# The four PSUM copies of a chunk step: engine chosen by the scheduler instead of fixed for each head

## Chip, cores and metric

One core of a Trainium2 chip runs the whole program. The metric is the device time of one execution in microseconds; before the change its median is 2306.48 us over 3 runs (2300.24 to 2307.2).

## What is computed

The reference is a two-layer backbone on 512 image tokens and 256 context tokens of width 1024. Layer 0 is an RWKV-7 mixer with 32 heads of 64 (16 pairs of heads) and two scan directions z, layer 1 a Hyena mixer with a long convolution. The change lies in the scan of layer 0, which for each head and direction is

```
def step(s, inp):
    r_t, w_t, k_t, v_t, a_t, b_t = inp
    sa = jnp.einsum('bhvk,bhk->bhv', s, a_t)
    s = s * w_t[:, :, None, :] + sa[..., None] * b_t[:, :, None, :] + v_t[..., None] * k_t[:, :, None, :]
    return s, jnp.einsum('bhvk,bhk->bhv', s, r_t)
```

over the context (256 tokens) and then the image (512), forwards for z = 0 and backwards for z = 1. All is float32.

## The kernel before

The scan is done in chunks of 64 tokens: 4 chunks of context and 8 of image, so 12 steps for each head. The coroutine `chain(r)` (line 1492) runs the 12 steps of a round `r`, which holds two pairs of heads, q = 0 and 1, with both directions z and both heads h of a pair: eight 64x64 problems side by side. There are 8 rounds, one after the other, so 96 steps in all. A step does this:

- eight matmuls of the operand `ar` with `sv` (state and values stacked) give `bx` in one PSUM bank (lines 1522 to 1524);
- two copies bring `bx` into `xs`, one for each head h (lines 1526 and 1527);
- eight matmuls of `xs` with the inverted triangular matrices `tt` give `bu` (lines 1536 to 1538), which two more copies bring into the lower or upper half of `sv[h]` (lines 1539 and 1540);
- eight matmuls of `sv` with `bt` give the state's increment `bs`, which the vector engine adds to the state `sc` and multiplies by the decay into the `sv` of the next step (lines 1541 to 1553);
- for image chunks, matmuls of `ar` and `arb` with `sv` give the output `by`, which `outputs` copies or adds to `yb`.

Both reads of a pair are of one bank: `quad("pa")` hands out half of PSUM bank 2. Head 0 lies in partitions 0 to 63, head 1 in 64 to 127.

Other coroutines run beside it. `fetch(p, g)` (line 1380) issues on SP the loads of the operands for pair p and group g, a group being four steps: 6 transfers `bk<-bkd`, 4 `ar<-ard` and 4 `ar<-zd` (zeros). Its ring `gring` has 4 places, two pairs of two groups; a place comes free after the fourth step of its group (lines 1559 to 1561). `prep(p, g)` (line 1418) makes from them the masked products `ar` and `arb` (vector engine) and the transposes `bt` (TensorE, evicted by ACT or the vector engine). `values` copies the values into the next `sv` (`sv<-vt`, ACT or POOL), `merge` makes `tt` from blocks of `inverse` (vector engine, tiles `lt` and `ltm`), `readout`, `operand` and `out_part` take a finished pair through the group norm (`s`, `yb`, `bo`), the split into `uh` and `ul` and the output projection with the weights `whi` and `wlo`; `adaln` works on the second layer's modulation (`aw`, `arow`).

The order of all instructions is written by a scheduler in the kernel, `run` (line 255). At each turn it takes from every live coroutine the next operation, estimates with `Model` (line 72) when its engine and its operands are free, and emits the one that can start first. An operation may come with alternatives (`alts`): then the way with the earliest estimated end is taken. `copy(eng, out, in_)` (line 403) gives an `ACTIVATE` on ACT (S) or a `COPY` on the vector engine (V); with a tuple of engines it gives alternatives. In `Model` any two accesses to one PSUM bank from different instructions wait for each other (line 120), and its prices and latencies are constants in the class. Every engine runs its instructions in the order in which they were emitted.

All operations are issued through one helper, so the profile has them all under line 58; tiles tell them apart.

Of the kernel before, what the change touches and what calls it, by code (L numbers as in the profile page):

```python
# [239 lines left out]
def net_kernel(ctx: ExitStack, tc: tile.TileContext, I, out, dbg=None):  # L240
    nc = tc.nc
    model = Model()
    V, S, T, G, SP = (Engine(e, n) for e, n in ((nc.vector, "V"), (nc.scalar, "S"), (nc.tensor, "T"), (nc.gpsimd, "G"), (nc.sync, "P")))
# [83 lines left out]
    def tl(pool, name, shape, bufs=1, dt=F32, tag=None):  # L327
        return model.new(pool, name, shape, bufs, dt, tag)
# [45 lines left out]
    def pt(kind):  # L374
        i = turn[kind]
        turn[kind] = (i + 1) % len(kinds[kind])
        return kinds[kind][i]

    def get(kind):

        return (yield from several(kind, 1))[0]
# [21 lines left out]
    def copy(eng, out, in_):  # L403
        if isinstance(eng, tuple):
            op = copy(eng[0], out, in_)
            op.alts = [op] + [copy(e, out, in_) for e in eng[1:]]
            return op
        if eng is S:
            return S.activation(out=out, in_=in_, func=AF.Copy)
        return eng.tensor_copy(out=out, in_=in_)  # L410
# [319 lines left out]
    HR = [slice(0, 64), slice(64, 128)]  # L730
# [568 lines left out]
    def rt(name, shape, bufs=1, dt=F32):  # L1299
        return tl(rx, name, shape, bufs, dt)  # L1300
# [14 lines left out]
    xs = rt("xs", [P, 2, 2, 2, C])  # L1315
# [13 lines left out]
    def two(a, b):  # L1329

        return slice(a, b + 1, b - a) if b > a else slice(a, b - 1 if b > 0 else None, b - a)
# [160 lines left out]
    def chain(r):  # L1492

        ps_ = 2 * r, 2 * r + 1
        QZH = [(q, z, h) for q in range(2) for z in range(2) for h in range(2)]

        def quad(kind):
            return pt(kind).rearrange("p (q z t) -> p q z t", q=2, z=2)

        while not all(p in pr for p in ps_):  # L1500
            yield
        gam, _, ptok = rounds[r]
        gf = gam.rearrange("p q c z -> p q (c z)")
        tt = [tts[p % len(tts)] for p in ps_]
        while not svs:
            yield
        sv, stok = svs.pop(0)
        for h in range(2):
            yield G.memset(sv[h][HR[h]], 0.0)
        sc = rt("sc", [P, 2, 2, C])  # L1510
        yield G.memset(sc, 0.0)
        for n in range(NC):
            g, i = divmod(n, 4)
            base, lc = BASE[g], (i, 3 - i)
            while not all((p, g) in grp for p in ps_):
                yield
            AR, ARB, BT, tok = zip(*[grp[p, g] for p in ps_])
            if n == 4:
                while yring.full():
                    yield  # L1520
                yb = tl(rv, "yb", [P, 2, NCX, C], YB), yring.take(), []
            bx = quad("pa")
            for q, z, h in QZH:
                yield T.matmul(bx[HR[h], q, z, :], lhsT=AR[q][z][h][:, 0, lc[z], :], rhs=sv[h][:, q, z, :], start=True, stop=True)

            for h, e in enumerate((S, V)):
                yield copy(e, xs[HR[h], h], bx[HR[h]])
            if g:

                by, ytok = yield from get("py")  # L1530
                by = by.rearrange("p (q z t) -> p q z t", q=2, z=2)
                for q, z, h in QZH:
                    yield T.matmul(by[HR[h], q, z, :], lhsT=sv[h][:, q, z, :], rhs=AR[q][z][h][:, 1, lc[z], :], start=q + z == 0, stop=False)
            while not all(p in mrgd for p in ps_):
                yield
            bu = quad("pa")
            for q, z, h in QZH:
                yield T.matmul(bu[HR[h], q, z, :], lhsT=tt[q][:, z, base[z] + lc[z], :], rhs=xs[:, h, q, z, :], start=True, stop=True)
            for h, e in enumerate((S, V)):
                yield copy(e, sv[h][HR[h]], bu[HR[h]])  # L1540
            if n < NC - 1:
                bs = quad("pn")
                for q, z, h in QZH:
                    yield T.matmul(bs[HR[h], q, z, :], lhsT=BT[q][z][:, lc[z], HR[h]], rhs=sv[h][:, q, z, :], start=True, stop=True)
                yield V.tensor_tensor(out=sc, in0=bs, in1=sc, op=ADD)
                while not svs:
                    yield
                nsv, ntok = svs.pop(0)
                gv = gf[:, :, two(2 * (base[0] + lc[0]), 2 * (base[1] + lc[1]) + 1)].unsqueeze(3).broadcast_to([P, 2, 2, C])
                for h in range(2):  # L1550
                    yield V.tensor_tensor(out=nsv[h][HR[h]], in0=sc[HR[h]], in1=gv[HR[h]], op=MUL)
                if n < NC - 2:
                    yield G.tensor_tensor(out=sc, in0=sc, in1=gv, op=MUL)
            if g:
                for q, z, h in QZH:
                    yield T.matmul(by[HR[h], q, z, :], lhsT=sv[h][:, q, z, :], rhs=ARB[q][:, h, z, lc[z], :], start=False, stop=q + z == 2)
                ys.todo.append((outputs, r, yb, by, ytok, base, lc, n - 4))
            stok[0] = True
            if i == 3:
                for t in tok:  # L1560
                    t[0] = True
            if n < NC - 1:
                sv, stok = nsv, ntok
        ttfree.update(ps_)
        ptok[0] = True
# [110 lines left out]
    def ready_merge(p):  # L1676
# [4 lines left out]
    ends = [reads, parts, Lane([(out_part, p) for p in range(0, NP, 2)], 1, lambda *a: bool(xp), OB)]  # L1681
    rr = range(NP // 2)
    scans = [Lane([(values, r) for r in rr], 1, lambda *a: True, B_VAL), Lane([(chain, r) for r in rr], 1, lambda *a: bool(zeroed), B_CHAIN),
             Lane([(merge, p) for p in range(NP)], 1, ready_merge, B_MERGE), ys, Lane([(fetch, *x) for x in order], 1, lambda *a: bool(zeroed)), Lane([(prep, *x) for x in order], W_PREP, lambda *a: True, B_PREP), invs]
    G2BIAS = 0
# [405 lines left out]
```

## Time and profile before

| | us |
|---|---|
| median of 3 runs | 2306.48 |
| the profiled execution | 2299.21 |
| its span | 2297.5 |
| busy in the span: TensorE | 2012.7 |
| vector engine | 1650.1 |
| ACT | 1067.1 |
| POOL | 371.8 |

The scan takes about a third of the span, from 835 to 1600 us. Before it lie the projections and the key side of layer 0, behind it the rest of the output projection, the filters and all of layer 1. A row of the timeline gives the start, the duration, the engine, what is written from what, how often in a row, and in brackets how long the engine stood idle before it and what ended that.

### The profile page before, as it was taken

How to read it: one execution, taken by the hardware profiler on the slowest of the kernel's cores; microseconds unless marked ns; L12 is line 12 of the kernel's file. 1: busy time of each engine (PE TensorE's matmuls, PEld its weight loads, DVE VectorE, ACT ScalarE, POOL GpSimd, SP SyncE). 2: the span in 40 equal slices, each digit the busy share in tenths (PEclk: the TensorE clock that was granted, in tenths of full speed). 3: DMA queues.
4: the chain of work that ended last, by engine and by line, in shares of the span. 5: the costliest groups of instructions: out<-in, count | busy, mean ns of one | idle time of the engine just before them, and what ended most of it. 6: DMA issues, size and time to landing. Idle time of an engine off the chain costs nothing. (4 is left out here: it accounts for less than half of the span.)

```text
span 2297.5 us, 53254 instructions
## 1 busy us (share of the span) xinstructions
PE 2012.7 (88%) x21678; PEld 1600.8 (70%) x21678; DVE 1650.1 (72%) x2624; ACT 1067.1 (46%) x1898; POOL 371.8 (16%) x574
## 2 busy tenths in 40 slices
PE   6699899998976787788988889888599999999997
PEld 2488777776754566676776767766477788878786
DVE  1956378999996869767576666766777576767676
ACT  2444588888762333345353453443453333333333
POOL 0400100000001322323223243221322000000000
PEclk8799999999988887999999999999799999999999
DMA  7055757795787884657566575543664423222232
GB/s 246 34 184 188 233 173 233 247 263 181 212 278 216 207 190 111 172 141 188 137 166 149 144 179 140 145 132 111 197 191 156 147 79 106 82 96 94 87 123 75
DMA packets 317628, 369.39 MB, mean 161 GB/s; under 512 B 132387, under 2 KB 203630, under 8 KB 317384
## 3 DMA queue, kind: packets, MB, share of 16 engines
q1 hardware_dynamic: 303752, 330.21, 49.3%
q0 software_dynamic: 13632, 35.78, 5.3%
q8 instruction: 171, 2.80, 0.5%
q14 instruction: 73, 0.60, 0.1%
HBM read 262.79 MB, written 102.30 MB: 159 GB/s over the span
## 5 line engine op out<-in xcount | busy, mean ns | idle before, releaser
L58 PE MATMUL ps<-m,whi 128*128 128x512 f32 (+1 forms) x1536 | 418.5, 374 | 47.7 <-ACT whi L58 19.0
L58 ACT ACTIVATE whi<-wraw 128x512 fp32r<-128x512 f32 x320 | 200.5, 628 | 385.4 <-PE ps L58 288.9
L58 DVE TENSOR_TENSOR wlo<-wraw,whi 128x512 fp32r<-128x512 f32 x320 | 229.6, 719 | 193.7 <-ACT whi L58 191.2
L58 PEld LDWEIGHTS ps<-m,whi 128*128 128x128 f32 x1536 | 262.4, 196 | 105.9 <-ACT whi L58 20.8
L58 PE MATMUL ps<-m,wlo 128*128 128x512 f32 (+1 forms) x768 | 245.8, 370 | 4.6 <-DVE wlo L58 4.5
L58 PE MATMUL ps<-ar,bk 128*64 128x64 f32 (+2 forms) x4096 | 216.7, 243 | 33.3 <-DVE ar L58 17.8
L58 PEld LDWEIGHTS ps<-ar,bk 128*64 128x64 f32 (+1 forms) x4096 | 184.6, 141 | 55.0 <-issue 24.5
L58 PE MATMUL ps<-h1h,whi 128*128 128x512 f32 x512 | 201.8, 394 | 2.4 <-ACT whi L58 1.4
L58 PE MATMUL ps<-h1h,wlo 128*128 128x512 f32 x512 | 201.2, 393 | 0.7 <-DVE wlo L58 0.7
L58 PE MATMUL ps<-h1l,whi 128*128 128x512 f32 x512 | 201.0, 393 | 0.0
L58 PEld LDWEIGHTS ps<-m,wlo 128*128 128x128 f32 x768 | 133.1, 196 | 31.1 <-DVE wlo L58 6.7
L58 DVE TENSOR_TENSOR ar<-ps,cst 64x512 f32<-64x512 f32 (+1 forms) x192 | 114.8, 599 | 22.9 <-PE ps L58 17.9
L58 POOL TENSOR_TENSOR sc<-sc,gam 128x256 f32<-128x256 f32 x80 | 56.4, 705 | 428.0 <-DVE sv L58 420.2
L58 PEld LDWEIGHTS ps<-h1h,whi 128*128 128x128 f32 x512 | 96.7, 189 | 22.1 <-ACT whi L58 1.8
L58 PEld LDWEIGHTS ps<-h1h,wlo 128*128 128x128 f32 x512 | 97.0, 189 | 21.1 <-DVE wlo L58 1.2
L58 PEld LDWEIGHTS ps<-h1l,whi 128*128 128x128 f32 x512 | 96.8, 189 | 20.0 <-DVE h1l L58 0.5
L58 PE MATMUL ps<-sv,bt 128*64 128x64 f32 x1408 | 89.1, 236 | 16.8 <-DVE sv L58 9.5
L58 DVE TENSOR_TENSOR ltm<-lt 128x90 f32<-128x90 f32 (+14 forms) x120 | 81.4, 678 | 29.2 <-DMA wraw<-wg 17.6
L58 ACT ACT_TABLE_LOAD x76 | 97.5, 1283 | 8.1 <-DMA aw<-ada_w 5.9
L58 PEld LDWEIGHTS ps<-sv,bt 128*64 128x64 f32 x1408 | 66.9, 142 | 41.8 <-DVE sv L58 15.8
L58 ACT ACTIVATE sv<-ps 64x256 f32<-64x256 f32 x96 | 36.1, 376 | 125.9 <-PE ps L58 122.2
L58 PE MATMUL ps<-xs,tt 128*64 128x64 f32 x1536 | 68.6, 232 | 28.2 <-DVE xs L58 26.0
(289 smaller groups left out, 4426.4 us busy)
## 6 DMA issues: line engine op xcount, KB each, us to landing
wraw<-wg SPq DMA_DIRECT2D x128, 256.0 KB
wraw<-w SPq DMA_DIRECT2D x128, 256.0 KB
aw<-ada_w SPq DMA_DIRECT2D x96, 256.0 KB
bkd<-bk SPq DMA_DIRECT2D x32, 768.0 KB
ard<-ar SPq DMA_DIRECT2D x32, 640.0 KB
ar<-ard SPq DMA_DIRECT2D x128, 128.0 KB
ar<-zd SPq DMA_DIRECT2D x128, 128.0 KB
wraw<-w_out SPq DMA_DIRECT2D x64, 256.0 KB
```

What stands on the lines that cost most here:

```text
L58: return getattr(self.eng.eng, self.fn)(*self.a, **self.k)
```

## The change

The fixed pair of engines (ACT for head 0, the vector engine for head 1) at both copies becomes a choice for each copy:

```
-            for h, e in enumerate((S, V)):
-                yield copy(e, xs[HR[h], h], bx[HR[h]])
+            for h in range(2):
+                yield copy((S, V), xs[HR[h], h], bx[HR[h]])
...
-            for h, e in enumerate((S, V)):
-                yield copy(e, sv[h][HR[h]], bu[HR[h]])
+            for h in range(2):
+                yield copy((S, V), sv[h][HR[h]], bu[HR[h]])
```

Nothing else is edited, but since the scheduler decides, the order of nearly all later instructions shifts. ACT in the first round, before the change, in three steps (`sv0` and `sv1` are the tiles of head 0 and 1, `ps2` the bank of `bx` and `bu`, `vt` the values):

```order
L58 ACTIVATE arow_7900<-ps7_70 128x128
L58 ACTIVATE xs_6590<-ps2_65 64x256
L58 ACTIVATE sv0_7185<-ps2_65 64x256
L58 ACTIVATE sv0_7989<-vt_6665 64x256
L58 ACTIVATE sv1_7990<-vt_6665 64x256
L58 ACTIVATE xs_6590<-ps2_65 64x256
L58 ACTIVATE m1_8018<-ps7_70 128x384
L58 ACTIVATE sv0_7850<-ps2_65 64x256
```

ACT at the same place after the change:

```order
L58 ACTIVATE xs_6590<-ps2_65 64x256
L58 ACTIVATE arow_7917<-ps7_70 128x128
L58 ACTIVATE xs_6590<-ps2_65 64x256
L58 ACTIVATE sv0_7185<-ps2_65 64x256
L58 ACTIVATE sv1_7186<-ps2_65 64x256
L58 ACTIVATE sv0_7985<-vt_6665 64x256
L58 ACTIVATE sv1_7986<-vt_6665 64x256
L58 ACTIVATE xs_6590<-ps2_65 64x256 x2
L58 ACTIVATE sv0_7850<-ps2_65 64x256
L58 ACTIVATE sv1_7851<-ps2_65 64x256
```

ACT now has both halves of each pair; once a foreign copy (`arow`) stands between them.

The vector engine a little earlier, in the second step of the round (`-` before, `+` after; `ltm` and `lt` belong to `inverse`, `sc` is the state of the same step):

```order
 L58 TENSOR_TENSOR ltm<-lt 128x174
 L58 TENSOR_TENSOR lt<-lt,ltm 128x3x2x29
-L58 COPY xs<-ps_65 64x256
 L58 TENSOR_TENSOR ltm<-lt 128x252
 L58 TENSOR_TENSOR lt<-lt,ltm 128x3x3x28
 L58 TENSOR_TENSOR ltm<-lt 128x324
-L58 STREAM_TRANSPOSE t_7794<-tt_6588 128x384
-L58 COPY sv_7178<-ps_65 64x256
+L58 STREAM_TRANSPOSE t_7799<-tt_6588 128x384
 L58 TENSOR_TENSOR lt<-lt,ltm 128x3x4x27
 L58 TENSOR_TENSOR ltm<-lt 128x390
```

Both copies are gone from the vector engine's queue there; the products of `inverse` stay, and `sc` and the next `sv` come behind them in both.

## Rows read from the trace of the kernel before

**Rows 1.** Stretches: stretch, length, busy us (instructions) per engine, clock, DMA share, GB/s.
```profile
835.00:1600.00 765.00, 658.34 (x13606) 531.53 (x13606) 537.31 (x1013) 321.09 (x651) 231.24 (x384) 0.94 0.59 147
```

**Rows 2.** Tile `sv`: durations ns min/median/max, first and last start us, forms.
```profile
L58 PE MATMUL ps<-sv,ar x1536: 219/222/371, 835.2 to 1594.3; 128*64 128x64 f32 x192
...
L58 ACT ACTIVATE sv<-vt x107: 400/413/419, 855.0 to 1583.1; 64x256 f32<-64x256 f32 x107
L58 ACT ACTIVATE sv<-ps x96: 358/377/379, 851.8 to 1596.6; 64x256 f32<-64x256 f32 x96
L58 DVE COPY sv<-ps x96: 420/427/430, 852.3 to 1597.4; 64x256 f32<-64x256 f32 x96
```

**Rows 3.** Timeline of one clean step at 1120 us.
```profile
1120.61 0.64 PE L58 MATMUL ps<-sv,ar 128*64 128x64 f32 x16
...
1121.29 0.38 ACT L58 ACTIVATE xs<-ps 64x256 f32<-64x256 f32 x1 [3.69 <-PE ps L58]
...
1121.70 0.43 DVE L58 COPY xs<-ps 64x256 f32<-64x256 f32 x1
...
1122.18 0.69 PE L58 MATMUL ps<-xs,tt 128*64 128x64 f32 x16
...
1122.91 0.38 ACT L58 ACTIVATE sv<-ps 64x256 f32<-64x256 f32 x1 [1.25 <-PE ps L58]
...
1123.32 0.43 DVE L58 COPY sv<-ps 64x256 f32<-64x256 f32 x1 [1.20 <-ACT sv L58]
```

**Rows 4.** Timeline of ACT and the vector engine in a step at 1382 us.
```profile
1382.46 0.38 ACT L58 ACTIVATE xs<-ps 64x256 f32<-64x256 f32 x1
...
1382.93 0.67 DVE L58 SCALAR_TENSOR_TENSOR bo<-bo,sg 128x512 f32<-128x512 f32 x1
1383.63 0.43 DVE L58 COPY xs<-ps 64x256 f32<-64x256 f32 x1
```

**Rows 5.** Timeline of ACT and the vector engine in the second step, at 857 us.
```profile
857.50 0.38 ACT L58 ACTIVATE xs<-ps 64x256 f32<-64x256 f32 x1 [1.06 <-PE ps L58]
...
862.67 0.25 DVE L58 TENSOR_TENSOR ltm<-lt 128x90 f32<-128x90 f32 x1 [6.45 <-DMA hkd<-hh]
...
864.05 0.43 DVE L58 COPY xs<-ps 64x256 f32<-64x256 f32 x1
```

**Rows 6.** Tile `xs`, columns as in rows 2.
```profile
L58 ACT ACTIVATE xs<-ps x96: 360/377/380, 836.0 to 1594.6; 64x256 f32<-64x256 f32 x96
L58 DVE COPY xs<-ps x96: 420/427/429, 836.4 to 1595.0; 64x256 f32<-64x256 f32 x96
```

**Rows 7.** Timelines of SP, vector engine, ACT and TensorE around one group boundary.
```profile
1455.05 1.78 SPq L58 DMA_DIRECT2D bk<-bkd  x3
...
1475.62 0.61 SPq L58 DMA_DIRECT2D ar<-zd  x1
...
1486.12 0.85 DVE L58 TENSOR_TENSOR sv<-sc,gam 64x256 f32<-64x256 f32 x2
...
1492.35 0.60 ACT L58 ACTIVATE bt<-ps 128x512 f32<-128x512 f32 x1 [0.77 <-PE ps L58]
...
1492.98 0.67 PE L58 MATMUL ps<-sv,ar 128*64 128x64 f32 x16
```

**Rows 8.** Timeline of ACT: a copy out of PSUM and the next one.
```profile
1100.27 0.38 ACT L58 ACTIVATE sv<-ps 64x256 f32<-64x256 f32 x1 [1.25 <-PE ps L58]
1100.55 0.49 ACT L58 ACTIVATE m<-ps 128x384 f32<-128x384 f32 x1
```

**Rows 9.** Groups of the vector engine, 835 to 1600 us: busy us, mean ns, idle before.
```profile
L58 DVE TENSOR_TENSOR ar<-ps,cst 64x512 f32<-64x512 f32 x124 | 85.3, 688 | 16.3 <-PE ps L58 13.2
...
L58 DVE COPY bt<-ps 128x512 f32<-128x512 f32 x18 | 12.2, 688 | 5.7 <-PE ps L58 5.5
```

**Rows 10.** Groups over the whole span, columns as in rows 9.
```profile
L58 POOL TENSOR_TENSOR sdl<-sf,sdh 128x512 fp32r<-128x512 f32 x16 | 21.3, 1334 | 45.7 <-ACT sdh L58 45.6
```

**Rows 11.** Waits from 835 to 1600 us: total us, times, longest us.
```profile
ACT arow L58 <- PE ps L58: 21.8, 13, 8.4
ACT whi L58 <- PE ps L58: 21.6, 20, 6.3
...
ACT yb L58 <- DVE yb L58: 7.1, 9, 2.9
...
ACT uh L58 <- DVE bo L58: 5.2, 7, 2.2
```

## Prediction

> **What bounds the kernel now.** I read the stages first, then the tiles of the recurrence, then single steps in the timeline.
>
> The table by stretches isolates the recurrence: from 835 to 1600 us, TensorE is busy 658 of 765 us, the vector engine 537 (70%), ACT 321 (42%) [rows 1]. No engine is full. The first matmul of a step starts at 835.2 and the last at 1594.3 [rows 2], so 96 steps take about 8 us each. The order of TensorE is the same in both kernels up to the first of these steps, and both leave the same work behind the last one (two sums and about 18 triples of the output projection). So the stage is what can change; a saving at its end moves all that follows forward.
>
> Inside a step, TensorE waits for two pairs of copies out of PSUM. In the clean step at 1120 us the ACT copy of `xs` starts at 1121.29 and takes 0.38, the vector copy starts at 1121.70, takes 0.43, and the next matmuls start at 1122.18; the pair of `sv` repeats this at 1122.91 and 1123.32 [rows 3]. **The two engines don't work side by side**: the second copy starts when the first has ended; both read one PSUM bank, and in the program the second waits for a semaphore of the first. From ACT's start to the end of the pair it is 0.41 + 0.43 = 0.84 us. So each pair is a serial piece of the recurrence, on two queues.
>
> Often it is longer. At 1382 us ACT starts `xs` at 1382.46, but the vector engine is in its queue's earlier work and starts its half at 1383.63 [rows 4]. At 857 us the wait is 6.5 us: the vector copy stands behind an `ltm` product that waited for a DMA [rows 5]. Counted over the 96 ACT and 96 vector copies of each tile (first and last in [rows 2, 6]), the vector copy starts 0.67 us after ACT's on average, against 0.41 in the clean step: 192 x 0.26 = 50 us of waiting in all.
>
> The steps are not the whole loop. The operands of four steps (a group, two pairs of heads) come through a ring that holds two groups. Their loads start on SP when the group two before has been read: for the group that starts at 1492.98, the loads run from 1455.05 to 1476.2, then the masks and transposes follow, with the last `bt` eviction at 1492.35 to 1492.95, and the recurrence starts right then [rows 7]. It had been ready since 1486.97, when its state products ended [rows 7]: 6.0 us of waiting for operands. So there are two interlocked loops: start of group n = start of group n-2, plus its four steps, plus load and preparation (1492.98 - 1455.05 = 37.9 us). **What a group's steps save counts once in two groups**, 12 times out of 24.
>
> **The change, part by part.** The order of instructions says what the scheduler chose. Of the 96 `xs` copies of each half, 161 of 192 now go to ACT and 31 to the vector engine; of the `sv` copies 177 and 15. That is 162 pairs wholly on ACT (153 of them back to back), 16 wholly on the vector engine and 14 mixed as before.
>
> *The pair.* No row shows two ACT copies of this shape in a row, but ACT's next eviction starts 0.28 us after such a copy: `sv` at 1100.27 takes 0.38 and `m` starts at 1100.55 [rows 8]. So a pair on ACT is 0.28 + 0.38 = 0.66 us instead of 0.84: 162 x 0.18 = 29 us less along the steps. The bounds are 0.76 (no overlap, 13 us) and 0.66; I take 0.66, because the row has the same shape and source. A vector pair is 2 x 0.43 = 0.86, no gain: 16 x 0.02 = 0.3 us, dropped. The mixed pairs stay.
>
> Had the halves run side by side before, a pair would have cost 0.43 us and ACT alone would lengthen it by 0.23: 162 x 0.23 = 37 us along the steps, half of it in the time, 2325. The clean step contradicts it [rows 3], and since the vector copy waits for ACT's semaphore in every pair, it gets no chance of its own. The Trainium skill (TensorEngine Tiling (Array Packing), PSUM Bottleneck) does advise evacuating PSUM with both ScalarE and VectorE; by that rule this change would go the wrong way, and the trace disagrees for two halves of one bank.
>
> *The vector engine's queue.* 162 of 192 pairs no longer pass it: 50 x 162/192 = 42 us at most, none at least. Not all of it goes. In the step at 857 us, the accumulation `sc` of the same step still stands behind the same `ltm` rows, as the order shows, so the stall moves from the copy to `sc`. I take half, 21 us.
>
> Together 50 us along 96 steps, 2.1 us per group. It counts 12 times: **25 us**.
>
> *Load on the engines.* ACT gains 146 copies at 0.38 us, 55 us [rows 2, 6], and 22 `sv<-vt` copies at 413 ns that went to POOL before, 9 us [rows 2]; 27 other evictions (`bt`, `tt`, `vt`, `arow`) leave it, some 11 us. The vector engine loses 146 copies at 427 ns, 62 us [rows 2, 6], and takes the 27 at up to 0.69 us each [rows 9], at most 19 us. So of 765 us ACT stands at about 321 + 55 + 9 - 11 = 374 and the vector engine at about 537 - 62 + 19 = 494. ACT's additions are hidden by its idle time before these copies; if that cover went, they would be paid in the steps (the slower rival below). The vector engine also does the preparation's masks (the long `ar` form alone is 85 us in this stage [rows 9]). It gets back 43 us in 96 steps, about 0.45 us a step; the preparation between the last load and the first step spans 1476 to 1493, two steps, so some 1 us per link, and I take half, as masks also wait for matmuls: 12 x 0.5 = **6 us**. Bounds 0 and 12.
>
> *The rest.* SP issues the same loads; the group's burst of about 21 us doesn't shrink. In the filter stage the scheduler's clocks come out shifted and four `sdl` subtractions go from POOL (1.33 us [rows 10]) to the vector engine, two `swl` the other way; at most 6 x 1.33 = 8 us either way, taken at 0 because matmuls and SP loads lie between them.
>
> **Sum.** 25 + 6 = 31 us off the profiled execution's 2299.2, so 2268. That execution stands 7.3 us below the median of the runs, 2306.5; 31 us off the median gives 2275.5, rounded to **2276 us**.
>
> **The rivals.**
>
> *Swallowed at the group boundary (no change).* If SP doesn't start the loads of group n earlier although group n-2 ends earlier, since weight loads stand ahead in its queue, each saving turns into a longer wait for operands like the 6.0 us at 1487. For it: SP issues one transfer after the other and also carries weights. Against: at 1455.05 the loads start with the last reading of the group before. Time: 2306.
>
> *Passed on in full.* If preparation isn't the limit in most groups, every step counts: 50 + 6 = 56 us, 2250. For it: within a group nothing but the steps decides. Against: the boundary at 1493 waits for `bt`.
>
> *ACT's queue becomes the bound (slower).* Place: nine of the ACT pairs have a foreign instruction between their halves, as the `arow` in the order: two `arow`, two `whi`, two `yb`, three `uh`. Each waits for something outside the step; the longest such waits before are 8.4, 6.3, 2.9 and 2.2 us [rows 11]. All at their longest: 2 x 8.4 + 2 x 6.3 + 2 x 2.9 + 3 x 2.2 = 42 us. If these pass on in full, no vector queue time comes back and the pairs give only their half of 29, the kernel is 42 - 15 = 27 us slower: 2333. It decides once these waits exceed about 15 us. Against: most waits of this kind are far below their longest (13 `arow` waits total 21.8 us [rows 11]), and the first half always stood in this queue.
>
> That the scheduler would keep the old engines is excluded by the counts above.
>
> **How the numbers follow.** 0.3% is about 7 us, what a measurement of this kernel tells from no change. The forecast has a chance of 0.52, in full 0.18, swallowed 0.14, slower 0.16. The first two are faster by over 0.3%: 0.70; the third is the same, the fourth slower. The forecast's own range is the queue term at 0 to 42 us and the preparation at 0 to 12: (29 + 0)/2 = 15 to (29 + 42)/2 + 12 = 48 us, 2259 to 2292. The range from 2246 to 2310 takes in the full and the swallowed case with a few us beyond them and leaves out the slower one.
>
> **What would show it.** Right: two ACT copies 0.28 us apart in each pair; ACT at about 374 and the vector engine at about 494 us in this stage; the first TensorE row of a step closer behind the copies; the stage some 31 us shorter, all else equal. If boundary waits grow beyond 6 us and the stage keeps its length, it is the second case. If ACT's waits inside a pair (before `arow`, `whi`, `yb`, `uh`) add up to tens of us, the slower case holds. The forecast is wrong too if the stage shortens and a later one grows by the same.

## The result, and the profile after

The changed kernel takes 2276.89 us (median of 4 runs, 2273.82 to 2283.02), the kernel before 2306.84 beside it (4 runs). The ratio is 0.9883, with a 95% interval from 0.9858 to 0.9907: 1.2% faster, 27 us by the ratio (21 to 33), 30 us between the two medians. The profiled execution of the changed kernel took 2273.82 us, its span 2272.1, which is 25.4 us less than the span before; the pieces below add up to these 25.4.

The recurrence between 835 and 1600 us, in the columns of [rows 1]:

```profile
835.00:1600.00 765.00, 655.23 (x13612) 528.32 (x13612) 489.66 (x901) 384.11 (x801) 226.48 (x365) 0.94 0.62 152
```

ACT has gained 63 us (321 to 384) and the vector engine lost 48 (537 to 490). The tile `sv` after gives the last step and the copies that moved [rows 2]:

```profile
L58 PE MATMUL ps<-sv,ar x1536: 219/222/369, 835.8 to 1577.9; 128*64 128x64 f32 x192
...
L58 ACT ACTIVATE sv<-ps x177: 377/379/382, 852.6 to 1581.2; 64x256 f32<-64x256 f32 x177
...
L58 ACT ACTIVATE sv<-vt x129: 400/414/419, 854.4 to 1565.5; 64x256 f32<-64x256 f32 x129
```

The steps begin where they did and end 16 us earlier (1577.9 against 1594.3). Cutting both spans at the start of the last step shows that this isn't all. Before, then after (stretch, length, busy us and instructions of PE, PEld, vector engine, ACT and POOL, clock, DMA share, GB/s):

```profile
835.20:1593.70 758.50, 653.16 (x13536) 527.86 (x13536) 532.76 (x1005) 318.07 (x644) 230.11 (x382) 0.94 0.59 148
1593.70:2297.50 703.80, 639.60 (x3008) 520.89 (x3002) 486.30 (x768) 259.61 (x433) 57.89 (x55) 0.96 0.38 121
```

```profile
835.80:1577.20 741.40, 645.60 (x13537) 523.64 (x13537) 481.33 (x888) 372.71 (x784) 221.61 (x360) 0.94 0.62 151
1577.20:2272.10 694.90, 635.85 (x3006) 516.92 (x3002) 480.88 (x768) 260.06 (x434) 55.09 (x53) 0.96 0.38 123
```

The stretch from the first step's start to the last's lost 17.1 us, and the part behind it, whose operations the change doesn't name, lost 8.9. TensorE runs the same number of products in the first stretch, to within one. Its idle time there fell from 105.3 to 95.8 us and its busy time from 653.2 to 645.6, so 9.5 of the 17.1 us are less waiting and 7.6 are the same products done in less time (more on that in the last section). What it waited for there, first before, then after (us in total, times, longest us):

```profile
PE ps L58 <- DVE xs L58: 26.0, 29, 7.1
PE ps L58 <- DVE sv L58: 16.0, 33, 2.2
...
PE ps L58 <- DMA ar<-zd: 7.5, 9, 2.4
...
PE ps L58 <- ACT sv L58: 6.0, 13, 0.6
```

```profile
PE ps L58 <- DVE sv L58: 20.0, 19, 9.7
PE ps L58 <- DMA ar<-zd: 15.4, 15, 2.0
...
PE ps L58 <- ACT xs L58: 6.3, 11, 1.0
...
PE ps L58 <- ACT sv L58: 4.0, 10, 0.6
PE ps L58 <- DVE xs L58: 1.0, 2, 0.6
```

The wait for the `xs` pair went from 26.0 to 7.3 us; the wait for `sv` (its copies, and the product with `gam` on the vector engine that begins the next step's `sv`) went from 22.0 to 24.0. The whole of what the copies could give TensorE was 48 us, and 31 of it are left: 16.7 us less. Its other idle time grew by 7.2 us, the wait for the zero loads `ar<-zd` by 7.9 alone, so that in all it fell by 9.5.

Two places show why so much copy time gives so little. First the `xs` pair at 1121 us of the changed kernel, on ACT and then on TensorE (start, length):

```profile
1121.64 0.78 ACT L58 ACTIVATE xs<-ps 64x256 f32<-64x256 f32 x2 [3.00 <-PE ps L58]
```

```profile
1121.82 0.39 PE L58 MATMUL ps<-whi,uh 128*128 128x512 f32 x1
1122.05 0.40 PE L58 MATMUL ps<-wlo,uh 128*128 128x512 f32 x1
1122.38 0.69 PE L58 MATMUL ps<-ar,sv 128*64 128x64 f32 x16
1122.89 0.64 PE L58 MATMUL ps<-xs,tt 128*64 128x64 f32 x16
```

The pair ends at 1122.42, but its product starts at 1122.89: TensorE's queue has the output projection and the step's output product (`ps<-ar,sv`) in front of it. TensorE lost nothing there, and in this order a shorter pair would have changed nothing.

Second, the long wait of the second step [rows 5], on TensorE before and after:

```profile
864.53 1.12 PE L58 MATMUL ps<-xs,tt 128*64 128x64 f32 x16 [7.07 <-DVE xs L58]
...
869.64 1.54 PE L58 MATMUL ps<-sv,ar 128*64 128x64 f32 x16 [0.47 <-DVE sv L58]
```

```profile
858.06 1.12 PE L58 MATMUL ps<-xs,tt 128*64 128x64 f32 x16 [0.86 <-ACT xs L58]
859.66 1.52 PE L58 MATMUL ps<-sv,bt 128*64 128x64 f32 x16 [0.48 <-ACT sv L58]
870.91 0.45 PE L58 MATMUL ps<-sv,ar 128*64 128x64 f32 x2 [9.73 <-DVE sv L58]
```

The product behind `xs` comes 6.5 us sooner, and the third step starts at 870.91 instead of 869.64: the accumulation `sc` stands behind the same `ltm` rows on the vector engine. After the change these start 3 us later than in [rows 5], behind another DMA (vector engine, changed kernel):

```profile
865.72 0.25 DVE L58 TENSOR_TENSOR ltm<-lt 128x90 f32<-128x90 f32 x1 [9.75 <-DMA wraw<-w_out]
...
869.89 0.42 DVE L58 TENSOR_TENSOR sc<-ps,sc 128x256 f32<-128x256 f32 x1
```

To follow the copies through all 96 steps I summed each piece of a step over them. The time from the first copy's start to the pair's end fell from 210.8 to 163.9 us (`xs` 110.8 to 82.5, `sv` 100.0 to 81.4). From a pair's end to the next product's start it rose from 29.0 to 51.2 us for `xs`; from the `sv` pair's end to the start of the last state product from 55.6 to 63.3, and from there to `sc` from 42.7 to 50.4, all of it in the second step just shown. So of 47 us that the copies lost, the time inside the steps lost 14.6.

### The profile page after: what moved, and what is told of

It reads as the page before. It is cut to its first block, busy times and chain, and to the rows that moved or that the text cites. A ratio compares the mean times of both kernels' runs of the same rounds, so it can differ in the third digit from the quotient of the medians.

```text
span 2272.1 us, 53272 instructions
## 1 busy us (share of the span) xinstructions
PE 2000.0 (88%) x21678; PEld 1591.7 (70%) x21678; DVE 1593.1 (70%) x2507; ACT 1122.1 (49%) x2039; POOL 360.1 (16%) x550
## 5 line engine op out<-in xcount | busy, mean ns | idle before, releaser
L58 PE MATMUL ps<-ar,bk 128*64 128x64 f32 (+2 forms) x4096 | 211.5, 242 | 48.5 <-DVE ar L58 18.7
L58 ACT ACTIVATE sv<-ps 64x256 f32<-64x256 f32 x177 | 67.0, 378 | 94.7 <-PE ps L58 91.3
L58 ACT ACTIVATE xs<-ps 64x256 f32<-64x256 f32 x161 | 60.8, 378 | 86.7 <-PE ps L58 84.9
L58 PE MATMUL ps<-sv,ar 128*64 128x64 f32 x1536 | 79.6, 234 | 21.9 <-DVE sv L58 19.8
```

Source lines behind the costliest of these rows:

```text
L58: return getattr(self.eng.eng, self.fn)(*self.a, **self.k)
```

## The experiments

The table cuts each profiled execution in three: the time inside steps; the waits between groups (at each fourth step, from the end of the product or copy that finishes it to the next step's first product, 23 times); and the tail from the last step's start to the end. Ratios are to the kernel before, from runs on the same chips. The medians of the result, of e1 to e8, of e9 to e11 and of e12 come from separate runs, beside which the kernel before had medians from 2303.55 to 2306.84 us; across these groups the ratios are what can be compared.

| kernel | median us | ratio, 95% interval | in steps | between groups | tail |
|---|---|---|---|---|---|
| before | 2306.84 | 1 | 649.9 | 108.6 | 703.8 |
| changed | 2276.89 | 0.9883 [0.9858, 0.9907] | 635.3 | 106.1 | 694.9 |
| e1 xs only | 2299.69 | 0.9980 [0.9967, 0.9993] | 657.8 | 112.4 | 694.2 |
| e2 sv only | 2304.80 | 0.9999 [0.9981, 1.0018] | 648.8 | 122.5 | 696.7 |
| e3 all on ACT | 2302.49 | 0.9988 [0.9975, 1.0001] | 634.4 | 135.7 | 697.1 |
| e4 exchanged | 2313.84 | 1.0030 [1.0012, 1.0049] | 659.5 | 123.6 | 699.8 |
| e5 before, filter | 2301.32 | 0.9992 [0.9972, 1.0012] | 653.0 | 106.8 | 701.6 |
| e6 changed, filter | 2281.53 | 0.9907 [0.9876, 0.9938] | 639.3 | 105.7 | 696.7 |
| e7 one copy | 2278.07 | 0.9881 [0.9851, 0.9910] | 591.6 | 159.0 | 694.6 |
| e8 latency | 2306.34 | 1.0004 [0.9983, 1.0024] | 620.1 | 131.3 | 693.5 |
| e9 changed, no zeros | 2251.41 | 0.9768 [0.9745, 0.9791] | 626.8 | 90.1 | 696.0 |
| e10 before, no zeros | 2297.63 | 0.9979 [0.9963, 0.9995] | 677.3 | 92.6 | 698.9 |
| e11 e7 and e9 | 2274.65 | 0.9866 [0.9844, 0.9889] | 626.4 | 118.0 | 699.0 |
| e12 before's order, ACT | 2285.57 | 0.9923 [0.9902, 0.9945] | 635.8 | 112.9 | 705.2 |

One profiled execution stands up to 12 us (e8) above or below its kernel's median, so a difference of a few us between two profiles can belong to the executions and not to the kernels.

**Parts of the change, e1 to e4.** From the changed kernel, e1 puts the second pair back, e2 the first; e3 and e4 replace the choice in both pairs:

```
e1:  for h, e in enumerate((S, V)): yield copy(e, sv[h][HR[h]], bu[HR[h]])
e2:  for h, e in enumerate((S, V)): yield copy(e, xs[HR[h], h], bx[HR[h]])
e3:  for h, e in enumerate((S, S)): ...
e4:  for h, e in enumerate((V, S)): ...
```

> Only the two xs copies go to the engine of choice; the sv copies are again one on ACT and one on the vector engine. Theory A (the gain is the time in which the second half waited for the vector engine's queue, plus 0.08 us of a pair): in the trace of the changed kernel the time from the first xs copy to the second fell by 24 us and the second copy itself by 4, against 14 and 4 for sv, so this kernel has 28 of the 46 us and its gain over the kernel before is about 28/46 of 30, 18 us: 2289. Rival B (the new order as a whole, not these copies, is the gain): any edit moves the filter stage and the boundaries of groups by several us either way, and the gain has no such share; it could be 0 or 30.

> Only the two sv copies go to the engine of choice; the xs copies are again one on ACT and one on the vector engine. Theory A: 18 of the 46 us along the steps, so about 12 us less than before, 2295; with the xs half's gain it adds up to the whole change, 30. Rival B: the two halves do not add up to 30.

> All four copies fixed on ACT, no choice. Theory A: 192 pairs on ACT instead of 162, so as the changed kernel or up to 5 us less, 2270 to 2280. Rival C (it is the choice that pays, and ACT's own queue costs when it gets everything): ACT has some 390 of 765 us and every pair then stands behind ACT's other work; 10 us or more over the changed kernel, 2287 or more.

> One fixed engine for each half as before, with the two engines exchanged: half 0 on the vector engine, half 1 on ACT. The pair still passes both queues and the first copy waits for the vector engine's queue. Theory A: no gain, within 8 us of the kernel before, since the pair is 0.43 + 0.38 us and its start waits where its second half waited. Rival B (reshuffle): the edit moves the order as much as the change does, and the time moves by 10 to 30 us.

The halves don't add up: about 5 us and none, where 18 and 12 were expected, and the whole is 30. In e1 the `xs` pair gained what it should (110.8 to 80.4 us over the steps), but the `sv` copies then waited 10 us more for the vector engine and the waits between groups grew. All on ACT gives some 3 us, not clear of none, though its copies are shorter still than the changed kernel's (149 us over the steps against 163.9) and its steps as short (634.4). The time is lost between groups. e4 ends 7 us over before (ratio 1.0030, clear of 1), within the 8 us of theory A and under the 10 of rival B. Its pairs are 45 us shorter over the steps (210.8 to 166.1), and its first copies start 45 us later behind the products that they read (20.7 to 65.8): the wait for the vector engine moved from the second half to the first. But e1 to e3 show that theory A isn't the only cause: rival B was right that edits of the same kind move the rest by as much. A reason is in the code: the scheduler picks every instruction by its clocks, and a copy on another engine shifts all that follows.

TensorE's waits in the steps of e3 show where its gain went; `xs` is as good as in the changed kernel:

```profile
PE ps L58 <- DVE sv L58: 32.8, 25, 9.5
PE ps L58 <- DVE arb L58: 13.2, 8, 5.5
...
PE ps L58 <- ACT xs L58: 5.2, 14, 0.9
```

The waits moved to the start of a step (`sv` with `gam`) and to the masks of the preparation (`arb`).

**The tail, e5 and e6.** The filter stage's subtractions and copies on the vector engine alone:

```
-    E_FL = (G,V)
+    E_FL = (V,)
```

> The kernel before, with the subtractions and copies of the filter stage that may go to POOL or the vector engine fixed on the vector engine. It asks where the 7 to 9 us come from that the changed kernel gains behind its last step: there four sdl subtractions moved from POOL to the vector engine. Theory D (POOL's 1.33 us subtractions were late in the chain of the filter stage): the tail from the last step to the end gets shorter than 703 us, by 5 to 10. Rival E (the tail is shorter because the whole order came out another way, and the place of these few operations is not it): the tail stays at 703 within 3 us or gets longer, as the vector engine takes all of them.

> The changed kernel with the same filter operations fixed on the vector engine. Theory D: the tail is 694 or up to 5 us shorter, the total 2270 to 2277. Rival E: the tail moves by as much as in the kernel before, in either direction, and the vector engine's load makes it longer.

The tail moves by 2 us either way, and neither time differs clearly from its parent's. The four `sdl` aren't what shortened the tail. It is 693 to 700 us in every other kernel of the table whose order differs from before, and 701.6 to 705.2 in the three that keep the order of before up to the last step (before, e5, e12): the tail's gain goes with the order, by an instruction that I haven't found.

**A shorter pair, e7.** One copy of 128 rows in place of two of 64:

```
-            for h in range(2):
-                yield copy((S, V), xs[HR[h], h], bx[HR[h]])
+            yield copy((S, V), xs[:, 0], bx)
...
-   lhsT=tt[q][:, z, base[z] + lc[z], :], rhs=xs[:, h, q, z, :]
+   lhsT=tt[q][HR[h], z, base[z] + lc[z], :], rhs=xs[HR[h], 0, q, z, :]
```

> The changed kernel with the two xs copies made one: a single copy of 128 x 256 from the bank into a dense xs, and the matmuls of the following product contract over the 64 rows of their head instead of 128 with zeros. In the profile of the changed kernel a pair of halves on ACT is 0.39 + 0.38 us; one copy of the same free size on 128 partitions should take 0.38. Theory A (the length of the copies stands on the recurrence's path): 0.39 us less in each of the 96 steps, 37 us along the steps. If it passes on as the gain of the change did (about 17 of 47 us in the stage), 14 us less, 2263; in full 2240. Rival F (TensorE's queue, which has other work placed ahead of the next product, or the boundaries of groups take it all): within 7 us of 2277.

Tile `xs` of this kernel: 96 copies in place of 192, each as long as a half was.

```profile
L58 ACT ACTIVATE xs<-ps x79: 361/384/387, 839.9 to 1590.4; 128x256 f32<-128x256 f32 x79
L58 DVE COPY xs<-ps x17: 406/424/425, 992.8 to 1565.5; 128x256 f32<-128x256 f32 x17
```

The steps lose 43.7 us, more than the 37 of the copies, and the waits between groups gain 52.9. Rival F holds: nothing passes on. Here the group boundary does what the prediction feared of the change: 21 of the 24 groups still start within 3 us of their own last `bt` eviction.

**TensorE's queue, e8.** One latency of the scheduler's model, from 0.28 to 0.08 us.

> The changed kernel with one number of the scheduler's model changed: it believes that TensorE can start 0.08 us after an ACT copy instead of 0.28, so it places less foreign work on TensorE's queue between a pair and the product that reads it. Theory G (of the 47 us that the copies lost, some 22 came back as TensorE work that stands ahead of the product after the xs pair, median 0.06 to 0.25 us): that gap falls again towards 0.06 and the stage gets 5 to 15 us shorter. Rival H (the work placed there has to be done by TensorE anyway and only moves): the gap falls, the stage stays within 5 us. Rival I: neither moves.

The gap between the end of the `xs` pair and its product fell only from 51.2 to 44.8 us. The steps got 15 us shorter, the waits between groups 25 longer, and the first step began at 847.4 instead of 835.8, since the number also governs what comes ahead. All of the change's gain is gone (this profiled execution stands 12 us below its median). This doesn't isolate the filler on TensorE; it shows once more what another order costs.

**Shorter loads, e9 to e11.** The zero fills of `ar` are left out and the preparation's products contract over 64 rows; e10 is the same on the kernel before, e11 on e7:

```
-   yield dma(out=AR[z][h][HR[1 - h], 0:na].rearrange("p a c t -> p a (c t)"), in_=zd[:, 0:na])
...
-   lhsT=bk[:, i, 1 - h, :], rhs=ar[h][:, 0:na, i, :]
+   lhsT=bk[HR[h], i, 1 - h, :], rhs=ar[h][HR[h], 0:na, i, :]
-   lhsT=bk[:, i, h, :], rhs=ar[h][:, 1, i, :]
+   lhsT=bk[HR[h], i, h, :], rhs=ar[h][HR[h], 1, i, :]
```

> The changed kernel without the eight loads per group that fill the unused half of each ar with zeros: the preparation's products now contract over the 64 rows of their head alone, so nothing reads those zeros. Theory J (22 or more of the 24 groups start right at the end of their last bt eviction, so half of the sum of steps, loads and preparation of two groups is the stage): the loads of a group lose 8 x 0.67 us on SP, 5.4 of some 27.7 us, and half of 22 x 5.4 = 118 us leaves the stage: 59 us, 2218. TensorE is busy for 645 us of the stage, which it can't fall below, so some of the 59 may come back as waiting for TensorE: 2218 to 2250. Rival K (SP has its transfers under way early enough and the end of the group two before sets the loads, so that fewer loads only end earlier): within 7 us of 2277.

> The same edit on the kernel before. Theory J: 59 us at most, 2247 to 2280, since the loop of loads and preparation sets the start of its groups too. Theory L (the copies' share of the change, half of some 16 us along the steps, stays, the rest of the change's gain was the order that came out): this kernel stands 8 us over the changed kernel with the same edit, not 30. Theory A: it stands 30 us over it.

> Both edits on the changed kernel: one dense xs copy a step, and no zero loads. The one copy took 31 us more off the steps between the start and the last first-product of a group (426 against 457.5) and gained nothing, as loads and preparation grew by as much. Theory J: with the loads 5.4 us shorter a group, the steps' saving counts half again, 16 us less than the changed kernel without zero loads: about 2205. Rival M (what grows when the steps shrink is work that has to be done anyway, on TensorE above all): no better than the changed kernel without zero loads.

The fastest kernel is e9: 2.3% below before, 1.2% below the changed one. Its waits between groups are 16 us shorter, but theory J's 59 us aren't there. The loads themselves did shrink (from the first `bk` to the last `ar` of a group 482 us over 22 groups instead of 609); then the preparation took longer behind them (370 us from the end of the loads to the last `bt`, against 275). SP's loads now wait for TensorE instead. What SP waited for TensorE in the steps (us in total, times, longest us), in the changed kernel and in e9:

```profile
SPq L58 <- PE ps L58: 105.6, 68, 10.8
```

```profile
SPq L58 <- PE ps L58: 204.1, 80, 18.3
```

On the kernel before the same edit gives only 0.2%: the waits between groups fall by 16 us as well, but the steps grow by 27. TensorE's waits there:

```profile
PE ps L58 <- DVE xs L58: 31.6, 24, 10.7
PE ps L58 <- DVE sv L58: 28.0, 33, 4.8
```

That is 60 us of waiting for a pair's second half or for `sv`, against 42 before; in e9, where most of these copies are on ACT, all waits for `xs` and `sv` are 31 us. It looks as if the vector engine's queue kept the loads from paying. But TensorE's idle time over the steps and boundaries of e10 is 92.3 us, 13 less than before. What grew is its busy time, from 653.2 to 677.6 us for the same number of products:

```profile
832.50:1602.40 769.90, 677.60 (x13543) 529.37 (x13544) 531.14 (x1002) 323.01 (x656) 228.17 (x375) 0.94 0.48 121
```

A part of this is a price of the edit itself, products of 64 rows among those of 128 (last section); in e9 the busy time grew too, by 3.6 us, at a higher clock. So it isn't shown why the loads pay on one kernel and hardly on the other: the vector engine's queue, that price and the order that came out aren't parted. e11 is no better than e9 (rival M).

**The engines alone, e12.** The plan of the kernel before is kept, and only the instruction written out differs:

```
             for h, e in enumerate((S, V)):
-                yield copy(e, xs[HR[h], h], bx[HR[h]])
+                o = copy(e, xs[HR[h], h], bx[HR[h]])
+                o.emit = copy(S, xs[HR[h], h], bx[HR[h]]).emit
+                yield o
```

and so for `sv`.

> The kernel before with its order kept: the scheduler plans as before, with the second half of each pair on the vector engine, and only when the instruction is written out is that half put on ACT. TensorE's order is that of the kernel before, row for row; ACT has 192 copies more and the vector engine 192 fewer, everything else stays where it was. It parts what the engines do from what the new order does. Theory A (the engines): TensorE waits 26.0 us for the xs pair and 22 us for sv in the stage of the kernel before, and 7.3 for the xs pair in the changed one; without a pass through the vector engine's queue some 19 us of the waits for xs and up to 10 of those for sv go, and the kernel takes 2277 to 2290. Theory N (the order: the two kernels' other instructions came out in another sequence, and that is the gain): within 5 us of the kernel before, 2300 to 2310. Rival C (ACT's queue, whose places were planned for one copy a pair, makes the pair late): over 2310.

This is the decisive run: 18 us, at a ratio clear of both 1 and e3's. Its stretches (as above) and TensorE's waits in the first of them:

```profile
834.90:1583.60 748.70, 654.89 (x13535) 530.94 (x13535) 453.94 (x815) 394.40 (x834) 231.54 (x382) 0.93 0.61 150
1583.60:2288.80 705.20, 637.88 (x3010) 520.42 (x3006) 484.94 (x766) 260.33 (x435) 57.95 (x55) 0.96 0.37 121
```

```profile
PE ps L58 <- DVE sv L58: 12.8, 22, 1.6
PE ps L58 <- ACT xs L58: 11.3, 15, 1.7
PE ps L58 <- ACT sv L58: 10.2, 18, 1.1
```

The tail is that of before (705.2 against 703.8), the steps are 14 us shorter, the waits for copies and `sv` fell from 48.0 to 34.3. This profiled execution took 2290.57 us, 5 above its median, that of before some 5 below, so the profiles show 9 of the 18 us. e3 has the same engine for these four copies and another order: the two ratios are 0.65% apart, 15 us, and the intervals don't meet. So another order can cost nearly all that the engines give. Between e12 and the changed kernel lie 9 us by the ratios and 12 by what each gained on its median (the two intervals, 0.9902 to 0.9945 and 0.9858 to 0.9907, just touch). That this is the gain of the order is a difference and not a measurement: the changed kernel's order with the old engines was not run, and 30 of its 192 pairs are not wholly on ACT. The profiles show where it would lie. TensorE's idle time in the first stretch is 93.8 us in e12 and 95.8 in the changed kernel, against 105.3 before: what the change saves there in waiting, e12 saves too. The changed kernel's stretch is 7.3 us shorter than e12's because TensorE is busy for 9.3 us less, and its tail is 10.3 us shorter.

## Why the prediction was right, and where it was wrong

The time was right (2276 against 2276.89), and most of the gain lies in the stage that was named. That the number came out so close is luck. The stage was to be 31 us shorter and lost 17.1, and another 8.9 came from the tail, a term taken at 0. In the sum, two terms were off in opposite ways and the step from copies to time failed.

- **The pair, 29 us.** A pair on ACT takes 0.78 us (the row at 1121.64), not 0.66: the second half starts when the first has ended. So the pairs themselves gave some 10 us (162 x 0.06), a little under the lower bound (0.76, 13 us).
- **The vector engine's queue, 21 of at most 42 us.** From the first copy's start to the second's, both pairs together lost 38.9 us (128.9 to 90.0), nearly the upper bound. The stall that the prediction named, at 857 us, did pass to `sc`; over the other steps the time up to `sc` did not grow, so it was the exception. Together the copies lost 46.9 us where 50 were forecast.
- **"50 along 96 steps".** This step failed. It took the time of a pair for the time of a step. TensorE filled most of a pair's length with other work: it waited 48 us in all for `xs` and `sv`, by the waits shown above, and got 16.7 of them back. The time inside the steps lost 14.6 us, a part of it TensorE's busy time. The product behind the `xs` pair did not come closer, as was to be seen if the forecast held: its gap grew from 29.0 to 51.2 us. The profile of before had the row that bounds this, and the prediction read the copies instead.
- **"What a group's steps save counts once in two groups".** Not so here: 14.6 us less in the steps and 2.5 less between groups make 17.1, so in these two profiles they counted in full; in e12 9.8 of 14.1 us did, in e7 none. The reading that groups start at their last `bt` holds: 23 of 24 do, before and after. What follows from it doesn't: load and preparation aren't of fixed length, since their TensorE and vector work stands in the same queues. They took 903 us over 22 groups before (first load to last `bt`) and 884 in the changed kernel, but 922 in e3 and 914 in e7.
- **Preparation, 6 us.** The waits between groups fell by 2.5 us, between its bounds of 0 and 12 and too little to tell from none.
- **The rest, 0 +- 8 us.** The tail gave 8.9. The term's cause was wrong too: with the filter operations pinned (e5, e6) the tail stayed within 2 us.
- **Load.** The vector engine stands at 489.66 (494 forecast), ACT at 384.11 (374).
- **The rivals.** Foreign instructions between the halves cost little: from start to start the nine pairs took 5.8 us more in all than pairs back to back, where the slower rival had 42. ACT waited 9.9 us for TensorE ahead of `arow`, with 2.2 the longest (21.8 and 8.4 in [rows 11]). The boundary that swallows is real, but for bigger savings (e7). The rival that was missing: the choice rewrites the whole order, and orders of this kernel differ by some 15 us.

## What to carry to other kernels

Price a shorter dependency by what the busiest engine waits for at that place, not by the dependency's length: 47 us off the copies took 16.7 us off TensorE's waits for them, because it had other work in its queue, and 9.5 off its idle time, because it then waited longer for other things. Where a scheduler writes the order, every edit is two changes; keep the order and swap only the engine to learn what the engine does (18 us here), and expect the reordering to be worth nearly as much (15 us between two orders with the same engine for these copies). Try an edit on both kernels: fewer loads gave 1.2% on the changed kernel and 0.2% on the one before, for a reason that these runs leave open.

## What the runs showed of the hardware

ACT's copies of the two halves don't overlap each other, while other neighbours on ACT do: `m` starts 0.28 us after a 0.38 us copy of the first half [rows 8], but the pair takes 0.78, and what follows its second half rarely starts early either (in 5 of 73 cases in e12). ACT in e12:

```profile
1096.60 0.78 ACT L58 ACTIVATE sv<-ps 64x256 f32<-64x256 f32 x2 [0.78 <-PE ps L58]
1097.40 0.49 ACT L58 ACTIVATE m<-ps 128x384 f32<-128x384 f32 x1
1097.84 0.60 ACT L58 ACTIVATE bt<-ps 128x512 f32<-128x512 f32 x1
```

The first half lies on rows 0 to 63, the second on 64 to 127, `m` and `bt` start at row 0; that the starting row decides is a guess, which no run isolates. The Trainium skill (ScalarE: Activation LUTs, What ACT_TABLE_LOAD costs) says that ACTIVATEs back to back overlap by about 93 ns; the trace agrees at [rows 8] (0.10) and disagrees for the halves.

Products of 64 rows among products of 128 rows cost TensorE time. The same 48 products, 32 of the preparation and 16 of the state, took 2.24 us before, where all contract over 128 rows, and 2.71 in e10, where the 32 contract over 64, both at the full clock (stretches before, then e10; the counts take in neighbours at the edges):

```profile
1483.77:1486.01 2.24, 2.24 (x55) 2.11 (x52) 0.85 (x3) 0.86 (x2) 0.00 (x0) 1.00 0.30 84
```

```profile
1470.32:1473.03 2.71, 2.71 (x55) 2.17 (x56) 0.94 (x4) 0.38 (x1) 0.00 (x0) 1.00 0.54 155
```

Over all steps at the full clock a state product right behind one of the preparation starts 0.20 us after it in e10 (median) and 0.06 before; the other way round it is 0.15 and 0.05. How much of e10's 24 us of added busy time this makes, no run isolates.

TensorE's granted clock is part of what an order costs. For some 13,540 products each TensorE is busy 645.6 us in the changed kernel and 659.9 in e3, at 0.94 and 0.93. Averaged over all executions of a kernel, the clock of the whole program was 0.943 in the changed kernel, 0.938 in e12 and 0.936 to 0.937 in the kernel before, and among the executions of one kernel those at a lower clock tend to be the longer ones. So some of what the changed kernel has beyond e12 may be the clock; no run parts the two. One place in e3, stretches of 4 us and TensorE's row in it:

```profile
1437.00:1441.00 4.00, 3.06 (x57) 2.28 (x52) 0.63 (x2) 1.72 (x5) 0.00 (x0) 1.00 1.16 229
1441.00:1445.00 4.00, 1.80 (x22) 1.64 (x24) 3.19 (x6) 0.20 (x1) 0.62 (x1) 0.70 0.64 141
1445.00:1449.00 4.00, 4.00 (x60) 3.50 (x59) 0.87 (x2) 1.31 (x4) 0.00 (x0) 0.50 0.53 152
1449.00:1453.00 4.00, 3.98 (x42) 2.75 (x40) 3.41 (x7) 1.78 (x5) 0.62 (x1) 0.95 0.04 10
```

```profile
1443.20 1.46 PE L58 MATMUL ps<-sv,ar 128*64 128x64 f32 x15 [2.87 <-DVE sv L58]
```

TensorE waits 2.87 us for `sv`; the clock then stands at 0.50, the lower of its two levels (1.2 GHz), while TensorE is busy again. Here a wait at a group's start was paid a second time.
